# Strassen steps for four of the eight K tiles of the two remaining output blocks in an MLP's down projection

## The chip, the cores and the metric

The kernel runs on one core of one Trainium2 chip, as one program. The metric is the device time of one execution in microseconds. The kernel before takes 2032.7 us (median of three runs, 2032.12 to 2035.39). One further execution was recorded by the profiler: it took 2031.86 us, and its instructions span 2030.0 us.

The engines are named as in the profile: PE is TensorE (PEld its weight loads), DVE is VectorE, ACT is ScalarE, POOL is GpSimd, SP is SyncE, whose queue issues nearly all loads.

## The reference

A decoder trunk with two layers over 256 positions and a model width of 2048, all in float32. Layer 0 has a gated short convolution, layer 1 a latent attention; each is followed by a squared-ReLU MLP with a hidden width of 8192 and by a DeepNorm layer norm. The change concerns the MLPs alone, of which there are two:

```python
def sq_relu_mlp(x, w1, w2):
    return jnp.square(jax.nn.relu(x @ w1)) @ w2

def reference(...):
    ...
        h = layer_norm(ALPHA * h + mix, ln_g[layer, 0], ln_b[layer, 0])
        h = layer_norm(ALPHA * h + sq_relu_mlp(h, mlp_w1[layer], mlp_w2[layer]),
                       ln_g[layer, 1], ln_b[layer, 1])
```

`x` is 256 x 2048, `w1` 2048 x 8192 and `w2` 8192 x 2048.

## The kernel before

**Precision.** Every operand of a matrix product is kept in two parts: a high part, a rounded copy made by ACT, and a low part, the difference made by DVE (`split`, L116 and L117). A product is then three matmuls, high x high, high x low and low x high (`dot`, L276 to L278). So every weight tile of 128 x 1024 that is loaded costs one ACT copy and one DVE subtraction before PE can use it.

**The MLP by stages.** The hidden width is cut into NQ = 8 stages of QC = 8 chunks of 128 (`mlp`, L557). In each stage q the *up* part makes the eight hidden chunks: `products` multiplies the activations by `w1`, `whole` (L332, L333) joins the parts of the result, ACT applies ReLU and square (L597, L598), and the chunk is split again (`put_split`, L337, L338). The *down* part multiplies the eight chunks, which are now eight K tiles, by `w2` and adds to the accumulator `acc`, 2 token halves x 2048 columns, taken as NB = 4 blocks of 512 columns. `put` (L581) adds one finished PSUM tile of 128 x 512 to a block of `acc` on DVE.

**Strassen in the stages q = 1 to 6 (`FAST`).** Two neighbouring K tiles, the two token halves and the blocks 0 and 1 make a 2 x 2 by 2 x 2 product. It is computed in Winograd's form with seven products in place of eight (`FACTORS`, `down_fast`). The left operands S1 to S4 are made from the hidden chunks on DVE (L605 to L608) and split into `forms`. The right operands T1 to T4 are made from the weights in `prepare`: two raw tiles hold the four sub-blocks, a third tile `raw_t` holds T1 and T3 (L149), T2 replaces a sub-block (L152), and T4 (L155) replaces another. The three tiles and half a tile for T4 are then split. The seven products accumulate in seven PSUM tiles over the four pairs of K tiles, and `combine` adds them to the four blocks and token halves with eleven DVE instructions and one ACT copy. Blocks 2 and 3 are computed plainly by `down`, a block at a time.

**What sets the order of the work.** All weight tiles stand in one list, `stream`, in the order of their use. `take` hands out the next tile and prepares tiles ahead of it (load, ACT copy, DVE subtraction), up to LOOK = 5 units, where a plain tile is one unit and a pair of Strassen tiles three (`size`). Raw tiles come from a pool of five buffers, high and low parts from pools of eight each. A load can start when a raw buffer is free, which is when DVE has made the low part from it. The order on each engine is fixed when the program is built; each engine takes its instructions in that order and waits where an operand or a buffer is not ready. PSUM has eight banks, used in rotation.

**Other places that the change touches.** `late_constants` loads the identity, the rotary tables and the mask after the convolution (L356 to L359). In the second MLP, `turn_residual` transposes the residual on PE and adds it to a block of `acc`, before the last block of stages 1 to 4. `to_out` loads the gain and bias of the last norm on POOL's queue (L914), computes the last down part, normalises and stores.

Of the kernel before, what the change touches and what calls it, by code (L numbers as in the profile page):

```python
# [16 lines left out]
P = 128  # L17
# [17 lines left out]
NB = 4  # L35
BW = D // NB
FAST = range(1, NQ - 1)
FIRST = (0, 1, 2, 4, 6, 8, 12, 16)
HEAD = 4
GROUP = 3  # L40
# [8 lines left out]

@with_exitstack  # L50
def trunk(ctx: ExitStack, tc: tile.TileContext, xT, vecs, w_first, w_in, w_out, w_kv, w_q, w_uk, w_uv,
          w_qn, w_qp, w_o, w1, w2, w2f, cosT, sinT, mask, ident, gb, out):
    nc = tc.nc
    PS = bass.MemoryType.PSUM
    const = ctx.enter_context(tc.tile_pool(name="const", bufs=1))
# [124 lines left out]
    def psum(name):  # L180
        return Banks.next().tile([P, 512], F32, tag="mm", name=name)
# [118 lines left out]
    def down_late(x, put, blocks):  # L300

        ws = {}
        for t in range(2):
            for n in blocks:
# [11 lines left out]
    def down_fast(x, forms):  # L316

        ps = {p: psum(f"ps_f{p}") for p, _, _ in FACTORS}
        n = len(x) // 2
        for j in range(n):  # L320
            b, = take(1)
            a = {"11": held(x[2 * j], 0), "12": held(x[2 * j + 1], 0), "22": held(x[2 * j + 1], 1)}
            for i in range(4):
                a[f"S{i + 1}"] = [forms[:, j, o, i * P:(i + 1) * P] for o in range(2)]
            for p, l, r in FACTORS:
                dot(ps[p], b[r], a[l], j == 0, j == n - 1)
        return ps

    def whole(ps, out):

# [8 lines left out]


    vec = const.tile([P, C_END], F32, name="vec")
    cos_t = const.tile([P, T], F32, name="cos_t")
    sin_t = const.tile([P, T], F32, name="sin_t")
    mask_t = const.tile([P, 3 * P], F32, name="mask_t")
    id_t = const.tile([P, P], F32, name="id_t")
    ones = const.tile([P, P], F32, name="ones")
    col = const.tile([P, 4], F32, name="col")
# [3 lines left out]
        nc.tensor.matmul(warm[:, :P], ones, ones, start=True, stop=True)  # L351
    nc.vector.memset(col[:, 0:1], 1.0 / D)
    nc.vector.memset(col[:, 1:2], 1.0 / RK)

    def late_constants():
        nc.sync.dma_start(id_t, ident)  # L356
        nc.sync.dma_start(cos_t, cosT)
        nc.sync.dma_start(sin_t, sinT)
        nc.sync.dma_start(mask_t, mask)  # L359

    def rsqrt(out, ve, amid=None):

# [169 lines left out]
    for m in range(NC):  # L532
# [17 lines left out]
        if m >= NC // 2:  # L550
            for k in range(2 * m - NC, 2 * m - NC + 2):
                ln.prepare(k)
    late_constants()
    ln.widen("a1", "a2")
    summed(ln, chain(products(1, z), lagged(NC - 1, z)), residual)

    def mlp(idx, ln, blocks, fast, begin=None, extra=None):  # L557

        xt = act.tile([P, NC, 2 * T], F32R, tag="b", name=f"xhl{idx}")
        xhl = [xt[:, k, :] for k in range(NC)]
        state["fast"] = fast
        todo = iter(range(NC))

        def normal():
            k = next(todo, None)
            if k is not None:
                ln.normal(k, xhl[k])  # L570

        def block(n, t):
            return acc[:, t, n * BW:(n + 1) * BW]

        def put(n, t, ps):
            if q == 0:
                nc.scalar.copy(block(n, t), ps)
                for _ in range(2):
                    normal()
            else:  # L580
                nc.vector.tensor_tensor(block(n, t), block(n, t), ps, ALU.add)  # L581

        for q in range(NQ):
            ht = act.tile([P, QC, 2 * T], F32R, tag="c", name=f"h{idx}_{q}")
            h = [ht[:, k, :] for k in range(QC)]
            forms = None
            if q in FAST:
                forms = act.tile([P, QC // 2, 2, 4 * P], F32R, tag="a2", name=f"forms{idx}_{q}")
            if q == NQ - 1 and begin:
                begin()  # L590
            pair = []

            def hidden(m, ps, evac, *func):
                f = tmp.tile([P, T], F32, tag="fh", name="fh", bufs=3)
                evac(ps, f, *func)
                if not func:
                    nc.scalar.activation(f, f, AF.Relu)  # L597
                nc.scalar.activation(f, f, AF.Square)  # L598
                put_split(h[m], f)
                pair.append(f)  # L600
                if forms is not None and m % 2:
                    (a11, a21), (a12, a22) = ((v[:, :P], v[:, P:]) for v in pair[-2:])
                    sf = fast.tile([P, 4, P], F32, tag="sf", name="sf")
                    s1, s2, s3, s4 = (sf[:, i, :] for i in range(4))
                    nc.vector.tensor_tensor(s1, a21, a22, ALU.add)  # L605
                    nc.vector.tensor_tensor(s3, a21, a11, ALU.subtract)
                    nc.vector.tensor_tensor(s2, s1, a11, ALU.subtract)
                    nc.vector.tensor_tensor(s4, a12, s2, ALU.subtract)  # L608
                    split(forms[:, m // 2, 0, :], forms[:, m // 2, 1, :], sf.rearrange("p i c -> p (i c)"))

            if q == 0:
                for m in range(QC):
                    if m < GROUP:
                        if m == 0:
# [12 lines left out]
                acc = act.tile([P, 2, D], F32, tag="a1", name=f"acc{idx}")  # L627
            else:
                for m, ps in enumerate(products(QC, xhl, turned=None if q == NQ - 1 and begin else TURNED)):
# [12 lines left out]
    def combine(put, p):  # L642

        put(0, 1, p["4"])
        put(0, 0, p["2"])
        put(1, 0, p["3"])
        v, u = (raws.tile([P, 2, BW], F32, tag="raw", name="vu")[:, i, :] for i in range(2))
        put(0, 0, p["1"])
        nc.scalar.copy(v, p["1"])
        nc.vector.tensor_tensor(v, v, p["6"], ALU.add)  # L650
        nc.vector.tensor_tensor(u, v, p["7"], ALU.add)
        put(1, 0, v)
        put(0, 1, u)
        put(1, 0, p["5"])
        put(1, 1, u)
        put(1, 1, p["5"])

    def to_wide(block, put, h):

# [28 lines left out]
    with tc.tile_pool(name="att", bufs=1) as ap:  # L688
        lat = act.tile([P, 2 * NK, 2 * T], F32R, tag="c", name="lat")
        chl, qhl = ([lat[:, k, :] for k in range(o, o + NK)] for o in (0, NK))  # L690
        kpe = ap.tile([P, 2, T], F32, name="kpe")
        nc.gpsimd.memset(kpe, 0.0)
        rc = ap.tile([P, 2], F32, name="rc")
# [4 lines left out]
        def rope(dst, src, rows):  # L698

            a = tmp.tile([P, T], F32, tag="sq", name="ropea")  # L700
            b = tmp.tile([P, T], F32, tag="nu", name="ropeb")
# [198 lines left out]
    summed(after, out_chunks(), residual)  # L900


    def turn_residual(block, n):
        if 0 <= n < NB:
            for t in range(2):
                ps = psum("turned")
                for j in range(4):
                    nc.tensor.transpose(ps[:, j * P:(j + 1) * P], xres[:, 4 * n + j, t * P:(t + 1) * P], id_t)
                nc.vector.scalar_tensor_tensor(block(n, t), ps, ALPHA, block(n, t), ALU.mult, ALU.add)
# [153 lines left out]
```

## Time and profile before

| what | us |
|---|---|
| median of three runs | 2032.7 |
| profiled execution | 2031.86 |
| its span, first to last instruction | 2030.0 |
| PE busy | 2022.8 |
| PEld busy | 1763.4 |
| DVE busy | 1637.1 |
| ACT busy | 1186.2 |
| stages q = 1 to 6 of the first MLP, each of the first five | 85.78 |
| stages q = 1 to 4 of the second MLP, with the turned residual | 86.67 to 86.69 |
| stages q = 5 and 6 of the second MLP | 85.78 |

Busy time is the union of an engine's recorded instructions. For PE it says little, since the records of pipelined matmuls overlap. The granted TensorE clock is 1.000 throughout. In a group's line, the names are the program's tiles (out<-in), then come the shape and the count, busy time and the mean length of one; a line number can be that of a helper that many callers share.

### The profile page before, as it was taken

To read this page: it belongs to the slowest core of one execution; us is meant where nothing else is said; L and a number is where in the kernel's file an instruction comes from. 1 tells how busy PE (TensorE), PEld (TensorE's weight loads), DVE (VectorE), ACT (ScalarE), POOL (GpSimd) and SP (SyncE) were. 2 spreads that over 40 slices of the span, in tenths; PEclk is the share of its full clock that TensorE was granted. 3 is DMA by queue.
4 is the path that set the end of the run, shared out by engine and by line. 5 is a ranking of instruction groups with operands and counts; after the bars stand their busy time and mean duration, and the time that the engine had idled before them with its cause. 6 is when DMAs were issued, how large, how long until landed. Compare 5 with 4: busy or idle time off the path is not lost.

```text
span 2030.0 us, 30192 instructions
## 1 busy us (share of the span) xinstructions
PE 2022.8 (100%) x11240; PEld 1763.4 (87%) x11240; DVE 1637.1 (81%) x2559; ACT 1186.2 (58%) x1849; POOL 4.5 (0%) x25
## 2 busy tenths in 40 slices
PE   9999999999999999999999999999999999999998
PEld 8888888988888888888889998898888888888886
DVE  7667677778898988989788978776889898898966
ACT  6444445676566565655656655566656656565661
POOL 0000000000000000000000000000000000000000
PEclk9999999999999999999999999999999999999999
DMA  8666666564746557465654544656474664746573
GB/s 307 209 191 187 188 190 193 162 210 138 251 148 216 193 170 256 145 229 174 232 176 153 177 129 137 195 168 205 136 240 155 213 204 164 250 143 221 190 228 121
DMA packets 106851, 385.32 MB, mean 190 GB/s; under 512 B 11856, under 2 KB 12752, under 8 KB 106448
## 3 DMA queue, kind: packets, MB, share of 16 engines
q1 hardware_dynamic: 105984, 381.17, 57.9%
q0 software_dynamic: 576, 2.10, 0.3%
q8 instruction: 88, 1.44, 0.3%
q14 instruction: 59, 0.48, 0.1%
q10 hardware_dynamic: 144, 0.13, 0.0%
HBM read 381.25 MB, written 2.10 MB: 189 GB/s over the span
## 4 chain that ended last, share of the span: by engine, by line
PE 99%; DMA 0%; DVE 0%; issue 0%; SPq 0%; ACT 0%; DVEq 0%
PE ps_u L192 20%; PE ps_l L192 13%; PE ps_u L196 11%; PE ps_d L276 7%; PE ps_d L277 7%; PE ps_d L278 7%; PE ps_l L196 7%; PE ps_f L278 4%; PE ps_f L276 4%; PE ps_f L277 4%; PE ps_w L226 1%; PE ps_w L224 1%; PE ps_w L225 1%; PE ps_g L226 1%; PE ps_g L224 1%; PE ps_g L225 1%
## 5 line engine op out<-in xcount | busy, mean ns | idle before, releaser
L117 DVE TENSOR_TENSOR lo<-raw,hi 128x1024 fp32r<-128x1024 f32 x710 | 858.7, 1222 | 271.5 <-ACT hi L116 199.9
L116 ACT CAST hi<-raw 128x1024 fp32r<-128x1024 f32 x710 | 740.9, 1050 | 428.4 <-DMA raw<-in_w_dram 134.6
L192 PE MATMUL ps_u<-xhl,hi 128*128 128x512 f32 x1792 | 621.3, 391 | 0.0
L196 PE MATMUL ps_u<-xhl,lo 128*128 128x256 f32 x1792 | 500.1, 280 | 0.0
L192 PEld LDWEIGHTS ps_u<-xhl,hi 128*128 128x128 f32 x1792 | 334.4, 187 | 71.9
L196 PEld LDWEIGHTS ps_u<-xhl,lo 128*128 128x128 f32 x1792 | 339.2, 189 | 1.7
L276 PE MATMUL ps_d<-hi,h 128*128 128x512 f32 x640 | 249.9, 390 | 0.0
L277 PE MATMUL ps_d<-lo,h 128*128 128x512 f32 x640 | 249.3, 390 | 0.0
L278 PE MATMUL ps_d<-hi,h 128*128 128x512 f32 x640 | 249.2, 389 | 0.0
L192 PE MATMUL ps_l<-xhl_a,hi 128*128 128x512 f32 x704 | 244.1, 393 | 0.0
L196 PE MATMUL ps_l<-xhl_a,lo 128*128 128x256 f32 x704 | 195.5, 280 | 0.0
L192 PEld LDWEIGHTS ps_l<-xhl_a,hi 128*128 128x128 f32 x704 | 132.2, 188 | 29.8
L278 PEld LDWEIGHTS ps_d<-hi,h 128*128 128x128 f32 x640 | 120.2, 188 | 25.2
L276 PEld LDWEIGHTS ps_d<-hi,h 128*128 128x128 f32 x640 | 120.2, 188 | 25.0
L277 PEld LDWEIGHTS ps_d<-lo,h 128*128 128x128 f32 x640 | 120.2, 188 | 24.6
L196 PEld LDWEIGHTS ps_l<-xhl_a,lo 128*128 128x128 f32 x704 | 131.9, 188 | 0.2
L597 ACT ACTIVATE fh<-fh 128x256 f32<-128x256 f32 x112 | 46.5, 415 | 89.2 <-DVE fh L333 89.1
L116 ACT CAST hi_t<-raw_t 128x1024 fp32r<-128x1024 f32 x48 | 50.6, 1054 | 55.5 <-DVE raw_t L149 30.5
L192 PE MATMUL ps_l<-z,hi 128*128 128x512 f32 x240 | 82.4, 391 | 0.0
L226 PE MATMUL ps_w<-xd,hi 128*128 128x258 f32 x256 | 72.7, 285 | 0.0
L224 PE MATMUL ps_w<-xd,hi 128*128 128x258 f32 x256 | 72.6, 284 | 0.0
L225 PE MATMUL ps_w<-xd,lo 128*128 128x258 f32 x256 | 72.4, 283 | 0.0
(253 smaller groups left out, 3185.1 us busy)
## 6 DMA issues: line engine op xcount, KB each, us to landing
raw<-in_w_dram SPq DMA_DIRECT2D x416, 512.0 KB, 4.3
raw<-in_w2f_dram SPq DMA_DIRECT2D x96, 512.0 KB, 3.5
raw<-in_w_in_dram SPq DMA_DIRECT2D x88, 512.0 KB, 3.8
raw<-in_w_out_dram SPq DMA_DIRECT2D x32, 512.0 KB, 3.6
raw<-in_w_o_dram SPq DMA_DIRECT2D x32, 512.0 KB, 4.0
raw<-in_w_kv_dram SPq DMA_DIRECT2D x10, 512.0 KB, 3.6
raw<-in_w_q_dram SPq DMA_DIRECT2D x8, 512.0 KB, 4.4
raw<-in_w_uk_dram SPq DMA_DIRECT2D x8, 512.0 KB, 4.6
```

The costliest lines, as they stand in the source:

```text
L116: nc.scalar.copy(hi, src)
L117: nc.vector.tensor_tensor(lo, src, hi.bitcast(F32), ALU.subtract)
L192: nc.tensor.matmul(ps, w[blk // 8][0][:, blk % 8, :], x, start=first, stop=False)
L196: nc.tensor.matmul(ps[:, :T], w[blk // 8][1][:, blk % 8, :], x[:, :T], start=False, stop=last)
L224: nc.tensor.matmul(ps[:, :W], hi, x[k][:, :W], start=k == 0, stop=False)
L225: nc.tensor.matmul(ps[:, :W], lo, x[k][:, :W], start=False, stop=False)
L226: nc.tensor.matmul(ps[:, :W], hi, x[k][:, W:], start=False, stop=k == NC - 1)
L276: nc.tensor.matmul(ps, x[0], w[0], start=first, stop=False)
L277: nc.tensor.matmul(ps, x[0], w[1], start=False, stop=False)
L278: nc.tensor.matmul(ps, x[1], w[0], start=False, stop=last)
L597: nc.scalar.activation(f, f, AF.Relu)
```

## The change

In the stages q = 1 to 6, blocks 2 and 3 are no longer all plain. Their first four K tiles (two pairs, `PLAIN = QC // 2 - 2`) are still multiplied plainly, both blocks side by side; the last four (two pairs) go through the same seven products as blocks 0 and 1, from a new copy of the weights, `w2g`. Per stage this replaces four of the eight plain tiles by two pairs of Strassen tiles.

The seven products are no longer combined in each stage. Products "2", "3", "4" and a fourth tile, "22", in which only plain matmuls accumulate, are added straight to `acc`; the plain matmuls of the first four K tiles accumulate in the same PSUM tiles as "2", "3" and "4" (`fast_products` then goes on adding there). Products "1", "6", "7" and "5" (`OWN`) are added to side sums, `sums`, of 4 x 2 x 512 columns, at q = 1 copied there by ACT. `fold` adds the side sums to `acc` once, by eight DVE instructions of 1024 columns among the up products of stage 7. Each fast stage has 15 additions to `acc` or `sums` (8 of them ACT copies at q = 1).

To make room, several tiles move: two neighbouring hidden chunks share one tile and are split by one ACT and one DVE instruction of 512 columns; the rotary tables and the mask are loaded at the start of the attention; the gain and bias of the last norm are loaded on SP's queue. `turn_residual` now turns one token half at a time, behind each of the first two pairs of plain tiles.

```diff
+PLAIN = QC // 2 - 2
...
             out += halves(w1[l, q * QC:(q + 1) * QC])
-            lead = 0
-            if q in FAST:
-                out += [(w2f[l, q, j, 0], w2f[l, q, j, 1]) for j in range(QC // 2)]
-                lead = 2
-            out += halves(w2[l, q, lead:])
+            if q not in FAST:
+                out += halves(w2[l, q])
+                continue
+            out += [(w2f[l, q, j, 0], w2f[l, q, j, 1]) for j in range(QC // 2)]
+            for j in range(PLAIN):
+                out += halves(w2[l, q, 3, j]) + halves(w2[l, q, 2, j])
+            out += [(w2g[l, q, j, 0], w2g[l, q, j, 1]) for j in range(QC // 2 - PLAIN)]
...
+    OWN = ("1", "6", "7", "5")
...
+    def fast_products(ps, x, forms, j, fresh, last):
+        b, = take(1)
+        a = {"11": held(x[2 * j], 0), "12": held(x[2 * j + 1], 0), "22": held(x[2 * j + 1], 1)}
+        for i in range(4):
+            a[f"S{i + 1}"] = [forms[:, j, o, i * P:(i + 1) * P] for o in range(2)]
+        for p, l, r in FACTORS:
+            dot(ps[p], b[r], a[l], p in fresh, last)
...
+        sums = fast.tile([P, 4, 2, BW], F32, name=f"sums{idx}")
+        def keep(p, g, ps):
+            at = sums[:, OWN.index(p), g, :] if p in OWN else \
+                block(*{"2": (2 * g, 0), "3": (2 * g + 1, 0), "4": (2 * g, 1), "22": (2 * g + 1, 1)}[p])
+            if q == 1 and p in OWN:
+                nc.scalar.copy(at, ps)
+            else:
+                nc.vector.tensor_tensor(at, at, ps, ALU.add)
+        def down_pairs(h, forms):
+            n = QC // 2
+            ps = {p: psum(f"ps_f{p}") for p, _, _ in FACTORS}
+            for j in range(n):
+                fast_products(ps, h, forms, j, ps if j == 0 else (), j == n - 1)
+            for p in ps:
+                keep(p, 0, ps[p])
+            ps = {p: psum("ps_d") for p in ("22", "3", "2", "4")}
+            for j in range(PLAIN):
+                for nb, two in ((3, ((1, "22"), (0, "3"))), (2, ((0, "2"), (1, "4")))):
+                    w, = take(1)
+                    for t, p in two:
+                        for kk in range(2):
+                            k = 2 * j + kk
+                            dot(ps[p], wide_rows(w, kk), held(h[k], t), k == 0, p == "22" and k == 2 * PLAIN - 1)
+                if extra and q <= NB and j < 2:
+                    extra(block, q - 1, j)
+            keep("22", 1, ps["22"])
+            for p in OWN:
+                ps[p] = psum(f"ps_f{p}")
+            for j in range(PLAIN, n):
+                fast_products(ps, h, forms, j, OWN if j == PLAIN else (), j == n - 1)
+            for p in ("3", "2", "4", *OWN):
+                keep(p, 1, ps[p])
+        def fold():
+            s1, s6, s7, s5 = (sums[:, i] for i in range(4))
+            c = acc.rearrange("p t (g b c) -> p t b g c", g=2, b=2)
+            for d, a, b in ((c[:, 0, 0], c[:, 0, 0], s1), (s6, s6, s1), (c[:, 0, 1], c[:, 0, 1], s6), (s7, s7, s6),
+                            (c[:, 1, 0], c[:, 1, 0], s7), (c[:, 1, 1], c[:, 1, 1], s7),
+                            (c[:, 0, 1], c[:, 0, 1], s5), (c[:, 1, 1], c[:, 1, 1], s5)):
+                nc.vector.tensor_tensor(d, a, b, ALU.add)
+                yield
...
             def hidden(m, ps, evac, *func):
-                f = tmp.tile([P, T], F32, tag="fh", name="fh", bufs=3)
+                both = pair_tile(m) if forms is not None else None
+                f = both[:, m % 2, :] if forms is not None else tmp.tile([P, T], F32, tag="fh", name="fh", bufs=3)
...
-                put_split(h[m], f)
-                pair.append(f)
-                if forms is not None and m % 2:
+                if forms is None:
+                    put_split(h[m], f)
+                elif m % 2:
+                    at = ht[:, m - 1:m + 1, :]
+                    split(at[:, :, :T], at[:, :, T:], both)
...
+                    if q == NQ - 1:
+                        next(folds)
...
-                combine(put, down_fast(h, forms))
-            for n in range(2 if q in FAST else 0, NB):
-                if n == NB - 1 and extra:
-                    extra(block, q - 1)
-                down(h, put, n)
+                down_pairs(h, forms)
+            else:
+                for n in range(NB):
+                    down(h, put, n)
...
-            nc.gpsimd.dma_start(gbt[:, n, :], gb[n].partition_broadcast(P))
+            nc.sync.dma_start(gbt[:, n, :], gb[n].partition_broadcast(P))
```

More of the change, by code (lines that the diff above doesn't have):

```diff
@@ L591, in mlp, with pair_tile @@
             pair = []
+            def pair_tile(m):
+                if m % 2 == 0:
+                    pool = (act, "ab") if m % 4 else (fast, "fp")
+                    t = pool[0].tile([P, 2 * T], F32, tag=pool[1], name="fp")
+                    pair.append(t.rearrange("p (i t) -> p i t", i=2))
+                return pair[-1]
             def hidden(m, ps, evac, *func):
-                f = tmp.tile([P, T], F32, tag="fh", name="fh", bufs=3)
+                both = pair_tile(m) if forms is not None else None
+                f = both[:, m % 2, :] if forms is not None else tmp.tile([P, T], F32, tag="fh", name="fh", bufs=3)
                 evac(ps, f, *func)
@@ L598, in hidden @@
                 nc.scalar.activation(f, f, AF.Square)
-                put_split(h[m], f)
-                pair.append(f)
-                if forms is not None and m % 2:
-                    (a11, a21), (a12, a22) = ((v[:, :P], v[:, P:]) for v in pair[-2:])
+                if forms is None:
[3 more added lines that the diff above has]
+                    split(at[:, :, :T], at[:, :, T:], both)
+                    (a11, a21), (a12, a22) = ((both[:, i, :P], both[:, i, P:]) for i in range(2))
                     sf = fast.tile([P, 4, P], F32, tag="sf", name="sf")
@@ L690, in trunk @@
         chl, qhl = ([lat[:, k, :] for k in range(o, o + NK)] for o in (0, NK))
+        cos_t = ap.tile([P, T], F32, name="cos_t")
+        sin_t = ap.tile([P, T], F32, name="sin_t")
+        mask_t = ap.tile([P, 3 * P], F32, name="mask_t")
+        for t, source in ((cos_t, cosT), (sin_t, sinT), (mask_t, mask)):
+            nc.sync.dma_start(t, source)
         kpe = ap.tile([P, 2, T], F32, name="kpe")
@@ L900, in trunk, with turn_residual @@
     summed(after, out_chunks(), residual)
[L903 to L909, printed above, removed]
+    def turn_residual(block, n, t):
+        ps = psum("turned")
+        for j in range(4):
+            nc.tensor.transpose(ps[:, j * P:(j + 1) * P], xres[:, 4 * n + j, t * P:(t + 1) * P], id_t)
+        nc.vector.scalar_tensor_tensor(block(n, t), ps, ALPHA, block(n, t), ALU.mult, ALU.add)
     def to_out(block, put, h):
```

44 lines of the change are left out of this document (7 added, 37 removed).

## The prediction

> **What bounds the kernel now.** I read four views in this order: the busy times and the chain of waits on the page, what TensorE (PE) waited for, one stage cut into three windows, and VectorE's (DVE's) timeline around a seam of that stage.
>
> ```profile
> span 2030.0 us, 30192 instructions
> PE 2022.8 (100%) x11240; PEld 1763.4 (87%) x11240; DVE 1637.1 (81%) x2559; ACT 1186.2 (58%) x1849; POOL 4.5 (0%) x25
> PE 99%; DMA 0%; DVE 0%; issue 0%; SPq 0%; ACT 0%; DVEq 0%
> ```
>
> The chain that ended last is 99% PE. Busy PE is no proof, since records of pipelined matmuls overlap; the waits are:
>
> ```profile
> PE offset L961 <- DVE udiag L959: 1.2, 1, 1.2
> PE warm L351 <- DVE col L353: 1.1, 1, 1.1
> PE ps_g L192 <- ACT hi L116: 0.6, 1, 0.6
> PE lnAB L376 <- DVE rr L371: 0.3, 1, 0.3
> ```
>
> PE waited 3.2 us in all and never in a fast stage, so a matmul removed there is worth its full pitch as long as PE still finds its operands ready. Pitch is read from starts, not from the modelled 0.39 us:
>
> ```profile
> 498.86 0.39 PE L276 MATMUL ps_f<-t,h 128*128 128x512 f32 x1
> 505.86 0.40 PE L276 MATMUL ps_f<-hi,h 128*128 128x512 f32 x1
> ...
> 699.79 0.39 PE L277 MATMUL ps_d<-lo,h 128*128 128x512 f32 x1
> 711.58 0.39 PE L278 MATMUL ps_d<-hi,h 128*128 128x512 f32 x1
> ```
>
> Thirty steps of the fast product take 7.00 us (233.3 ns each), 52 plain steps 11.79 us (226.7 ns). A Strassen step is not only fewer matmuls: each is 6.6 ns dearer.
>
> ```profile
> 671.40:690.98 19.58, 19.58 (x86) 15.76 (x85) 18.37 (x25) 12.54 (x18) 0.00 (x0) 1.00 0.60 196
> 690.98:712.78 21.80, 21.80 (x99) 18.12 (x98) 19.32 (x24) 10.66 (x12) 0.00 (x0) 1.00 0.77 255
> 627.00:671.40 44.40, 44.40 (x257) 39.09 (x256) 36.80 (x58) 29.00 (x50) 0.00 (x0) 1.00 0.51 164
> sum 85.78, PE 85.78 PEld 72.97 DVE 74.49 ACT 52.20 POOL 0.00; mean PE 28.59 PEld 24.32 DVE 24.83 ACT 17.40 POOL 0.00
> ```
>
> The columns are stretch, length, then busy time of PE, PEld, DVE, ACT, POOL, granted clock (1.00), DMA share, GB/s. One fast stage (q = 3 of the first MLP) is 44.40 us of up products, 19.58 of fast products for blocks 0 and 1, and 21.80 of plain products for blocks 2 and 3. DVE is busy 74.49 of 85.78 us: 11.29 us of slack, the quantity on which all depends.
>
> **The sum.** *Matmuls.* A pair of K tiles of blocks 2 and 3 costs 24 plain matmuls, 24 x 226.7 = 5.44 us; by a Strassen step 21 matmuls, 21 x 233.3 = 4.90. That saves 0.54 us a pair, 1.08 a stage (2 pairs), and **13.0 us** for 12 stages. Neither the four plain tiles' new order nor the interleaved order in which the changed program issues the second half's products is in the trace. Should the 576 plain matmuls that stay take 233.3, that costs 3.8 us; should the 504 new Strassen matmuls take 226.7, it gains 3.3. I keep the rates of their own kinds.
>
> The Trainium skill (TensorE: Matmul & The Clock Gate, "Back-to-back issue gap") gives N/2.4 + 2.5 ns, 215.8 ns at 512 columns. By that the 72 matmuls would be worth an estimated 15.5 us and the two kinds would cost the same; the rows show 226.7 and 233.3, and the measurement decides.
>
> *DVE.* Two plain tiles of a pair need two low-part subtractions of 1.222 us. The Strassen pair needs three (L117), one raw_t (1.225), two half-size combinations (0.688, 0.690) and the T4 low part (0.686): 6.96 against 2.44, so 4.5 us more a pair and 9.0 a stage. Summed durations overrun busy time, because consecutive instructions overlap: one stage's add up to 82.1 against 74.49, a factor 0.907. So 8.2 us more. Splitting two hidden chunks at once (0.686 for 2 x 0.421, four times) gives back 0.3 to 0.6; I take 0.3. The accumulations stay 15 a stage (7 + 1 + 7 for 11 + 4), half of which now go to side sums; at q = 1 eight of them become ACT copies. New DVE work: 74.5 + 8.2 - 0.3 = **82.4 us** against a PE stage of 85.78 - 1.08 = 84.70. The slack falls from 11.3 to 2.3 us, 97% busy. ACT gains 2 x (1.05 + 0.62) us on 52.2 and stays near 55.
>
> *The seam.* Let E be the end of the fast products of blocks 0 and 1 (690.98 above).
>
> ```profile
> 688.08 0.68 DVE L581 TENSOR_TENSOR acc<-acc,ps_f 128x512 f32<-128x512 f32 x1
> 689.79 1.23 DVE L117 TENSOR_TENSOR lo<-raw,hi 128x1024 fp32r<-128x1024 f32 x1 [1.03 <-ACT hi L116]
> 690.93 0.68 DVE L581 TENSOR_TENSOR acc<-acc,ps_f 128x512 f32<-128x512 f32 x1
> 691.53 1.22 DVE L117 TENSOR_TENSOR lo<-raw,hi 128x1024 fp32r<-128x1024 f32 x1
> 692.66 1.28 DVE L581 TENSOR_TENSOR acc<-acc,ps_f 128x512 f32<-128x512 f32 x2
> ```
>
> Between these starts a 512-element instruction takes 0.60 us of the queue and a 1024-element one 1.14. The two accumulations from 692.66 on and three more end at 692.66 + 5 x 0.60, about E + 4.7. Then, in the changed program's order, come the first three steps of pair A (2.9 us, to E + 7.5) and the accumulation of product "22", which the third plain tile finishes at E + 2 x 2.72 + 1.36 = E + 6.8. Behind it stand pair A's remaining preparations: its second low part ends at E + 10.5, T4's high part (ACT) at E + 11.8, its low part at E + 12.8. PE arrives at E + 48 x 0.2267 = E + 10.9, begins with products that need the former, and wants T4's high part at E + 11.4. So it stalls 0.4 to 0.5 us; pair B then follows within a few tenths. Where the residual is turned (second MLP, q = 1 to 4), both sides shift by 0.9 us of transposes and 1.2 of DVE. I charge **0.45 us a stage, 5.4 us in all**; the ends are 0 and the 3.4 of the last rival but one. The wait on "22" has the rest of DVE's queue behind it. The skill states the reason in the same page ("Architectural detail": ACT and DVE are strict FIFO); the timeline above agrees, with DVE idle 1.03 us before a low part while a finished product waited.
>
> *What costs nothing.* The deferred folding is 8 instructions of 1.22 us in q = 7's up products (about 10 us a MLP): q = 7 needs no Strassen operands, so its DVE work is about 40 of 44.4 us; without that cover it would cost up to 20 us. The constants' loads move to a point where SP's queue has five tiles in flight. The gain/bias loads move from POOL's queue to SP's behind the last up product, ahead of the last four weight tiles: 2 MB at about 250 GB/s is 8 us, and PE reaches those tiles some 27 us later (3 half-blocks of 10.9 and 5.4 us), so nothing is late; the end of the program keeps its DVE tail.
>
> Sum: 2031.86 (the profiled execution; span 2030.0) - 13.0 + 5.4 = 2024.3. The median of the runs, 2032.7, is 0.8 above that execution, so I forecast **2025.1 us**.
>
> **Rivals.** *Clean overlap:* PE never stalls, since its product order at the seam is already bent around T4. For it: no wait in any stage before. Against: slack falls to a fifth. 2032.7 - 13.0 = 2019.7 us. *Balance:* stalls of 0.75 to 1.4 us a stage eat most of the saving, which is what a DVE at 98 to 99% would give: 2028.6 to 2036.8 us, middle 2032. *DVE becomes the bound:* one mechanism, the weight preparation of the fast stages. DVE lags some 7 us at the start of a stage's up products (five tiles, three and four accumulations after pair B) and must recover this out of idle time. Much of the old 11.3 us is waiting for tiles that PE has yet to free, and vanishes when DVE is late; the part in which ACT waits for a raw tile's load does not, since a late DVE frees the raw buffer late too. The stage takes 82.4 us plus what remains of idle time; beyond 3.4 us remaining, the kernel is slower than before. With 4.3 remaining, 86.7 a stage, +0.9 x 12 = 2043 us. For it: in the stage above ACT waited 9.8 us for such loads. Against: 5.8 of them lie in the plain stretch, where DVE had little else to do. *Not what it says:* were the new fast products priced like plain ones with one per pair still spared, the saving would be 16.3, within the range's low end.
>
> **How the numbers follow.** Forecast with stalls under 0.75 us 0.35, clean overlap 0.25: faster 0.60. Balance 0.22, DVE-bound 0.18. About 0.2% (4.1 us) is what a measurement here can tell from no change. The low end, 2017.5, takes in clean overlap and part of the 3.3 us on the fast pitch; the high end, 2037.5, takes in balance and leaves out most of the DVE-bound case. The likeliest case's own range is 2019 to 2028.6.
>
> **What would show it.** Right: matmuls of 512 columns fall by 72; the second half's 42 fast matmuls take 9.8 us; DVE is busy 82 to 83 us of a fast stage of 85.1; PE waits under 0.75 us a stage, on the T4 parts of pair A or B. Wrong: fast stages at or above 85.8 us, PE waiting on low parts of pairs in the first half too, or DVE idle over 3 us a stage in waits for ACT's high parts and for loads while PE waits.

## The result, and the profile after

The changed kernel takes 2041.87 us (median of six runs, 2040.30 to 2044.38), the kernel before 2031.98 beside it: a ratio of 1.0046 (95% interval 1.0033 to 1.0059). It is 9.9 us slower; the forecast was 7.6 faster, and 2041.87 lies above the range. The profiled execution took 2041.51 us, with a span of 2039.7. All 9.7 us of added span lie in the twelve fast stages: 2.2 in the first MLP (517.12 for 514.93) and 7.5 in the second (525.75 for 518.28). Here and below, times of a kernel are medians, and figures of stages, waits and single instructions are those of its one profiled execution.

Busy times and the chain of waits on the page of the changed kernel:

```profile
span 2039.7 us, 29958 instructions
PE 2019.8 (99%) x11168; PEld 1746.3 (86%) x11168; DVE 1730.4 (85%) x2631; ACT 1214.2 (60%) x1853; POOL 2.3 (0%) x21
PE 72%; DVE 18%; DMA 5%; issue 3%; ACT 2%; SPq 0%; ACTq 0%; DVEq 0%
```

There are 72 matmuls fewer, as forecast, and 93 us more of DVE work. Busy time doesn't show the loss; the chain does: PE's share fell from 99% to 72%. What PE waited for in the second MLP's six stages, and then in the first's:

```profile
PE ps_d L279 <- ACT t L119: 2.0, 3, 0.8
PE ps_u L195 <- ACT hi L119: 2.0, 1, 2.0
PE ps_f L279 <- DVE acc L584: 1.8, 1, 1.8
```

```profile
PE ps_d L279 <- ACT t L119: 3.5, 5, 0.8
PE ps_d L280 <- DVE t L120: 0.5, 1, 0.5
```

The `t` that ACT writes is T4's high part. This view names only the longer waits. By the matmuls' starts (gaps over 0.15 us beyond the pitch) PE lost 6.8 us in the first MLP and 10.4 in the second, and none before. One stage (q = 6 of the first MLP) in three windows (up products, blocks 0 and 1, blocks 2 and 3), with the columns as in the prediction:

```profile
885.43:929.85 44.42, 44.42 (x258) 39.15 (x257) 41.60 (x60) 31.46 (x49) 0.00 (x0) 1.00 0.62 217
929.85:949.41 19.56, 19.56 (x86) 15.68 (x85) 18.78 (x26) 12.05 (x17) 0.00 (x0) 1.00 0.63 189
949.41:971.80 22.39, 21.47 (x93) 16.95 (x92) 21.41 (x26) 10.81 (x12) 0.00 (x0) 1.00 0.50 163
sum 86.37, PE 85.45 PEld 71.78 DVE 81.79 ACT 54.32 POOL 0.00; mean PE 28.48 PEld 23.93 DVE 27.26 ACT 18.11 POOL 0.00
```

The part that lost six matmuls grew from 21.80 to 22.39 us. E, the start of PE's first matmul for blocks 2 and 3, is at 949.41:

```profile
949.17 0.40 PE L281 MATMUL ps_f<-hi_t,forms 128*128 128x512 f32 x1
949.41 0.40 PE L279 MATMUL ps_d<-hi,h 128*128 128x512 f32 x1
```

DVE's timeline in this part:

```profile
950.16 1.23 DVE L120 TENSOR_TENSOR lo<-raw,hi 128x1024 fp32r<-128x1024 f32 x1 [1.26 <-ACT hi L119]
951.30 1.28 DVE L584 TENSOR_TENSOR acc<-acc,ps_f 128x512 f32<-128x512 f32 x2
952.50 2.47 DVE L584 TENSOR_TENSOR sums<-sums,ps_f 128x512 f32<-128x512 f32 x4
954.89 1.22 DVE L120 TENSOR_TENSOR lo<-raw,hi 128x1024 fp32r<-128x1024 f32 x1
...
957.88 0.68 DVE L584 TENSOR_TENSOR acc<-acc,ps_d 128x512 f32<-128x512 f32 x1
...
960.75 0.69 DVE L158 TENSOR_TENSOR raw<-raw 128x512 f32<-128x512 f32 x1
```

ACT's and PE's timelines there:

```profile
961.52 0.62 ACT L119 CAST t<-raw 128x512 fp32r<-128x512 f32 x1 [1.24 <-DVE raw L158]
```

```profile
960.39 0.39 PE L279 MATMUL ps_d<-hi,h 128*128 128x512 f32 x1
960.89 0.50 PE L280 MATMUL ps_d<-lo,h 128*128 128x512 f32 x1
962.20 0.50 PE L279 MATMUL ps_d<-t,h 128*128 128x512 f32 x1 [0.81 <-ACT t L119]
```

DVE adds the first half's products until E + 5.5 and starts to make T4 at E + 11.3, ACT's high part ends at E + 12.7, and PE, which by the forecast wanted it at E + 11.4, starts at E + 12.8, having lost 1.1 us there and 0.3 on the matmul before.

### The profile page after: what moved, and what is told of

It is laid out like the page before. It is cut to its first block, busy times and chain, and to the rows that moved or that the text cites. A ratio compares the mean times of both kernels' runs of the same rounds, so it can differ in the third digit from the quotient of the medians.

```text
span 2039.7 us, 29958 instructions
## 1 busy us (share of the span) xinstructions
PE 2019.8 (99%) x11168; PEld 1746.3 (86%) x11168; DVE 1730.4 (85%) x2631; ACT 1214.2 (60%) x1853; POOL 2.3 (0%) x21
## 4 chain that ended last, share of the span: by engine, by line
PE 72%; DVE 18%; DMA 5%; issue 3%; ACT 2%; SPq 0%; ACTq 0%; DVEq 0%
PE ps_u L195 16%; PE ps_l L195 13%; PE ps_u L199 8%; PE ps_l L199 7%; DVE lo L120 6%; DMA raw<-in_w_dram 4%; PE ps_d L279 4%; PE ps_d L281 4%; PE ps_d L280 3%; DVE lo_t L120 2%; DVE raw_t L152 2%; PE ps_w L229 1%; PE ps_w L227 1%; PE ps_w L228 1%; ACT hi L119 1%
## 5 line engine op out<-in xcount | busy, mean ns | idle before, releaser
L279 PE MATMUL ps_d<-hi,h 128*128 128x512 f32 x472 | 184.9, 392 | 0.5 <-ACT hi L119 0.3
L280 PE MATMUL ps_d<-lo,h 128*128 128x512 f32 x472 | 184.6, 391 | 0.3
L281 PE MATMUL ps_d<-hi,h 128*128 128x512 f32 x472 | 184.0, 390 | 0.0
L119 ACT CAST hi_t<-raw_t 128x1024 fp32r<-128x1024 f32 x72 | 75.7, 1051 | 129.4 <-DVE raw_t L152 113.3
L279 PEld LDWEIGHTS ps_d<-hi,h 128*128 128x128 f32 x472 | 88.6, 188 | 21.0 <-ACT hi L119 1.8
L280 PEld LDWEIGHTS ps_d<-lo,h 128*128 128x128 f32 x472 | 88.6, 188 | 20.8 <-DVE lo L120 2.5
L281 PEld LDWEIGHTS ps_d<-hi,h 128*128 128x128 f32 x472 | 88.6, 188 | 18.4
L152 DVE TENSOR_TENSOR raw_t<-raw,raw 128x1024 f32<-128x1024 f32 x72 | 87.6, 1217 | 7.0 <-DMA raw<-in_w2f_dram 7.0
L120 DVE TENSOR_TENSOR lo_t<-raw_t,hi_t 128x1024 fp32r<-128x1024 f32 x72 | 87.7, 1219 | 2.4 <-ACT hi_t L119 1.9
L195 PE MATMUL ps_l<-z,hi 128*128 128x512 f32 x240 | 82.4, 391 | 0.0
L645 ACT ACTIVATE fp<-fp 128x256 f32<-128x256 f32 x96 | 39.9, 416 | 68.7 <-DVE fp L334 68.6
L229 PE MATMUL ps_w<-xd,hi 128*128 128x258 f32 x256 | 72.7, 285 | 0.0
```

What stands on the lines that cost most here:

```text
L119: nc.scalar.copy(hi, src)
L120: nc.vector.tensor_tensor(lo, src, hi.bitcast(F32), ALU.subtract)
L152: nc.vector.tensor_tensor(t.rearrange(two, a=2), b12.unsqueeze(1).to_broadcast([P, 2, BW]), r1.rearrange(two, a=2), ALU.subtract)
L195: nc.tensor.matmul(ps, w[blk // 8][0][:, blk % 8, :], x, start=first, stop=False)
L229: nc.tensor.matmul(ps[:, :W], hi, x[k][:, W:], start=False, stop=k == NC - 1)
L279: nc.tensor.matmul(ps, x[0], w[0], start=first, stop=False)
```

## The experiments

Three theories stand against each other. **Queue:** PE waits for the DVE and ACT work of the Strassen operands (a variant: DVE is simply full). **Banks:** in stages 1 to 4 of the second MLP the two turned tiles and the second half's eight share eight PSUM banks (the second half is the work on blocks 2 and 3), so that a product waits until DVE has emptied another's bank. **Pace:** the up products, on which the diff changes nothing, run at either of two paces, 346.7 or 353.3 ns for a pair of a 512- and a 256-column matmul (44.39 or 45.2 us an up part), without any wait. Stages 1 to 7 of the two MLPs have fourteen such parts, twelve of them in the fast stages. Before, all ran at the first pace; in the changed kernel four ran at the second (q = 2 of the first MLP, q = 3, 4 and 5 of the second). Each time below stands beside its ratio to the kernel before, with the 95% interval.

**e1, one pair in place of two.**

```diff
-PLAIN = QC // 2 - 2
+PLAIN = QC // 2 - 1
```

> PLAIN is 3 instead of 2: only one pair of K tiles of blocks 2 and 3 takes the Strassen step, everything else of the change stays. Queue theory (TensorE starves because VectorE's queue, 97% busy, brings the operands of the seam too late): VectorE falls to about 78 of 85 us a stage, TensorE's waits fall to under 0.3 us a stage, and the saving of 36 matmuls (6.5 us) comes through: 2026 to 2029 us. Pace theory (the loss lies in TensorE, whose matmuls run at a longer pitch in the new mix whatever VectorE does): half of the saving and half of the loss go, so the time lies half way between the two kernels, 2035 to 2039 us.

2041.69 us, 1.0048 (1.0033 to 1.0063). Gaps fell from 17.2 to 6.2 us in all, but ten of the fourteen up parts now ran at 353.3, for four: six more, 6 x 0.82 = 4.9 us. With the 6.5 us of matmuls that are not saved, this takes back the 11.0 us of the gaps. Neither expectation held, because both moved at once.

**e2, the residual turned at the end of the stage.**

```diff
-                if extra and q <= NB and j < 2:
-                    extra(block, q - 1, j)
+            for t in range(2):
+                if extra and q <= NB:
+                    extra(block, q - 1, t)
```

> The residual is turned after the second half's products instead of between its plain tiles, so that no more than eight PSUM tiles are open there. Bank theory (in stages 1 to 4 of the second MLP ten tiles share eight banks, and TensorE waits for the release of product 3): waits on accumulations go from stages 2 and 3 of the second MLP, 3 to 6 us, so 2036 to 2039 us, all of it in the second MLP. If the banks play no part: 2040 to 2043 us, and stages 2 and 3 of the second MLP stay above 89 us.

2034.65 us, 1.0014 (1.0004 to 1.0023). By the median, the place of eight transposes a stage is worth 7 us, more than was expected. The trace doesn't show where: the profiled execution (2038.35 us) was 3.7 slower than the median, and its second MLP took 525.81 us, as in the changed kernel. There the up products behind the transposes waited 3.0 us for DVE's additions. The first MLP, which the edit leaves alone, had gaps of 3.8 us for 6.8: single executions differ by that much.

**e3, without the low parts of the left operands.**

```diff
-                    split(at[:, :, :T], at[:, :, T:], both)
+                    nc.scalar.copy(at[:, :, :T], both)
```

> Leaves out a part of the computation: in stages 1 to 6 the low parts of the hidden chunks and of the S operands are not made, and TensorE reads the high part in their place. TensorE's instructions stay the same in number and size, VectorE loses eight instructions of 512 columns a stage, about 4.8 us of its queue, and no load or buffer is touched. Queue theory: TensorE's waits fall to under 0.4 us a stage and the matmuls saved come through, 2020 to 2027 us. Pace theory: nothing that TensorE does has changed, 2039 to 2043 us.

2030.12 us, 0.9991 (0.9982 to 1.0001). With less on DVE the first MLP's gaps fall from 6.8 to 1.2 us. The second MLP keeps 4.5 us in stages 2 and 3, of which 1.4 are waits for DVE's additions and 2.2 a wait of the next up part for its first weight tile. This fits the queue theory, but can't tell a full DVE from one late operand.

**e4, three additions for T1 to T4 on GpSimd.**

```diff
-        nc.vector.tensor_tensor(t4, b21, b12, ALU.subtract)
+        nc.gpsimd.tensor_tensor(t4, b21, b12, ALU.subtract)
```

(and the two others likewise)

> The three additions that make the T operands (L152, L155, L158) run on GpSimd, which is idle, instead of VectorE, which loses six times 2.3 us a stage, about 14 us, and comes to 67 of 85 us. Queue theory, if GpSimd takes no more than about twice VectorE's time for them: 2019 to 2024 us, since VectorE's load is the cause. Rival: GpSimd is slower than that (over 14 us a pair) or slows VectorE when both run, and its results become what the seam waits for: 2045 us or more.

2203.88 us, 1.0849 (1.0824 to 1.0873). Groups of instructions of this kernel (count, then busy time and mean ns):

```profile
L152 POOL TENSOR_TENSOR raw_t<-raw,raw 128x1024 f32<-128x1024 f32 x72 | 203.8, 2831 | 1222.8 <-DMA raw<-in_w2f_dram 622.0 <-DVE fp L334 424.3 <-DMA raw<-in_w2g_dram 121.7
L120 DVE TENSOR_TENSOR t<-raw,t 128x512 fp32r<-128x512 f32 x72 | 97.6, 1355 | 0.0
L584 DVE TENSOR_TENSOR sums<-sums,ps_f 128x512 f32<-128x512 f32 x80 | 49.4, 678 | 0.0
```

GpSimd takes 2831 ns where DVE took 1217, and T4's low part on DVE grows from 682 to 1355 ns in the mean. That mean hides two cases: 36 of the 72 ran wholly beside a GpSimd instruction and took 2033 ns, the other 36 took 677. The additions of PSUM tiles took 678 beside GpSimd (30 of them) and 677 without it. PE waited 80 us for T4's low part and 22 for its high part; the granted clock was 0.975 here. The Trainium skill ("SBUF — State Buffer", "SBUF: two separate sides") says that GpSimd and a DVE instruction with two SBUF inputs take one port pair from each other for a whole instruction. The trace agrees: 2033 for 677 ns with two SBUF inputs, 678 for 677 with a PSUM input.

**e5, the pace alone, in the kernel before.**

```diff
-                for m, ps in enumerate(products(QC, xhl, turned=None if q == NQ - 1 and begin else TURNED)):
+                for m, ps in enumerate(products(QC, xhl, turned=None)):
```

> The kernel before with one edit: in the stages 1 to 6 of both MLPs the up products no longer swap the high and the low matmul of the third K tile. Same matmuls, same operands, same DVE and ACT work; only the order of two matmuls in each of twelve up parts differs. Pace theory (the up products run at 346.7 or at 353.3 ns a pair, set by how PE enters the part; 128 pairs, so 0.85 us a part): if the swap is what brings them to 346.7 after the even 227 ns of the plain products, the twelve up parts take 45.2 us and the time is 2032.0 + 12 x 0.85 = 2042. If the even 227 ns entry alone does it, 2032.0. Queue theory (every microsecond over the forecast is a wait of PE for DVE or ACT): 2032.0, as no wait changes.

2042.32 us, 1.0049 (1.0032 to 1.0066). The order of two matmuls in each of thirteen up parts (the edit reaches stage 7 of the second MLP too), with no wait added, costs 10 us. All thirteen ran at the longer pace. The same stage as in the prediction (q = 3), by windows:

```profile
627.78:672.99 45.21, 45.21 (x257) 39.23 (x256) 38.19 (x59) 29.14 (x49) 0.00 (x0) 1.00 0.54 175
672.99:692.50 19.51, 19.51 (x87) 15.84 (x86) 17.34 (x24) 12.43 (x17) 0.00 (x0) 1.00 0.60 182
692.50:714.30 21.80, 21.80 (x98) 18.01 (x96) 19.46 (x23) 10.91 (x11) 0.00 (x0) 1.00 0.75 250
```

With 257 records in the up part in both kernels, a clock of 1.00 and PE busy throughout, the up part takes 45.21 us for 44.40. The pace is shown by itself, 0.81 us a part.

**e6, the swapped K tile elsewhere in each stage** (on e1).

```diff
+                at = {1: TURNED, 2: None, 3: 7, 4: 1, 5: 3, 6: 4} if idx == 1 else {1: None, 2: 5, 3: 6, 4: 8, 5: 9, 6: 12}
```

> The kernel with one pair of Strassen steps in blocks 2 and 3 (measured at 2041.7, ten of its twelve up parts at 353.3 ns a pair), with the swapped K tile of the up products at another place in each stage: 2, none, 7, 1, 3, 4 in the first MLP and none, 5, 6, 8, 9, 12 in the second. Pace theory: the up parts that the swap brings to 346.7 are 0.85 us shorter, the others stay at 45.2 us; 2041.7 less 0.85 for each, so 2033 to 2041, and the trace tells which places do it. Queue theory: the waits, 6.2 us in all in the kernel with one pair, set the time, 2041 to 2042 whatever the place.

2042.73 us, 1.0054 (1.0040 to 1.0069). In the first MLP the part without a swap behind a Strassen pair fell to 44.38 us; those with swaps at 7, 1, 3 and 4 stayed at 45.2. Behind plain products it is the reverse: with the swap 44.39, without it 45.21. In the second MLP, where the turned residual stands in between, swaps at 8 and 9 gave 347.1 ns a pair, those at 5, 6 and 12 about 353. So the swap doesn't bring one pace; it can also take PE out of the better one. The time lies above the range of the pace theory, which had let the swap only help.

**e7, the residual turned among the up products.**

```diff
-                if extra and q <= NB and j < 2:
-                    extra(block, q - 1, j)
...
+                    elif extra and q <= NB and m in (3, 5):
+                        extra(block, q - 1, (m - 3) // 2)
```

> The changed kernel, with the turned residual of the second MLP moved out of the plain products of blocks 2 and 3 into the up products of the same stage (behind products 3 and 5), where no Strassen tile holds a bank. Nothing is left out. Bank theory (the two turned tiles and the eight tiles of the second half share eight banks, so that products wait for DVE's additions): the waits of 4.6, 2.5 and 2.2 us in the second MLP go and the time is 2033 to 2036, below or near that of turning them at the end of the stage (2034.7). Queue theory: DVE has the same work, so only what the banks had cost can go; waits of 0.5 to 1.9 us a stage stay in the first MLP, sum near 6.8 us. Pace theory: the transposes among the up products can bring the rest of a part to another pace, 0 to 0.6 us in each of four stages.

2034.03 us, 1.0007 (0.9998 to 1.0016). The second MLP's gaps fall from 10.4 to 4.2 us, the first's from 6.8 to 5.4. Stages 2 and 3 go from 7.1 us of gaps to 0.25. So the place of the transposes is what cost them; the banks are a part of it, as the account below shows.

**e8, the change without its Strassen steps.**

```diff
-PLAIN = QC // 2 - 2
+PLAIN = QC // 2
```

(and `fold` for blocks 0 and 1 alone, with half the columns)

> The changed kernel without its Strassen steps in blocks 2 and 3: all eight K tiles are multiplied plainly there, the two blocks side by side, the four side sums are still kept and folded for blocks 0 and 1. It has as many matmuls as the kernel before, so none of the 13.0 us are saved; DVE has four additions and the two extra pairs' splits and sums less than the changed kernel. Queue theory: PE waits for nothing, 2032 to 2034. Pace theory: the up parts are entered from the even 227 ns of the plain products, as before, all at 346.7, so 2032 to 2034 too. Bank theory: the turned residual shares banks with eleven tiles here as well, so 0.5 to 2 us a stage in four stages of the second MLP, 2034 to 2040.

2035.13 us, 1.0014 (1.0004 to 1.0023). All up parts ran at 346.7, with gaps of 1 us in all. The time lies in the range of the bank theory, but its waits do not appear: the second MLP's gaps are 0.2 us. The profiled stages are 1.3 and 1.0 us longer per MLP than before: about 3 us is the price of side sums, half the fold and interleaving, and the larger loss belongs to the Strassen steps.

**e9, blocks 2 and 3 in the order in which operands are made** (on the changed kernel; T4's product last).

```diff
+    AS_MADE = tuple(sorted(FACTORS, key=lambda f: "3175264".index(f[0])))
...
-            for p in ("3", "2", "4", *OWN):
+            for p, _, _ in AS_MADE:
```

> The changed kernel with one edit: in blocks 2 and 3 the seven products of a pair are issued in the order in which DVE and ACT make their operands (3, 1, 7, 5, 2, 6, and 4, which needs T4, at the end), and are added to the sums in that order. No work is added or left out. Seam theory (PE waits because product 4 comes first and needs T4, which is made last; the rest of DVE's work would fit): the need for T4 moves 18 matmuls x 233 ns = 4.2 us back, the eight waits on T4's high part (5.6 us) and the smaller ones beside them go, the first MLP's six stages fall from 517.1 to 511-514 us, and the time is 2033 to 2037, as the banks of the second MLP stay as they are. Rival, DVE bound (DVE is late by its whole load, whatever product asks first): the waits move to other products, 2040 to 2043. Pace theory: some up parts may be entered in another pattern, up to 0.85 us each either way.

2040.11 us, 1.0040 (1.0027 to 1.0054). By the total, the full DVE (the rival, 2040 to 2043) seemed right. By stages it is not: in the first MLP's stages 1 to 5 PE waits nowhere, and its gaps fall from 6.8 to 0.8 us, with DVE's load unchanged. Its six stages take 513.3 us, as the seam theory expected. Five of its up parts now run at 353.3 in place of one (+3.3 us), and the second MLP keeps 10.2 us of gaps.

**e10, the same order on e7.**

> The same order of products in blocks 2 and 3, on the kernel whose turned residual stands among the up products (2034.0). Seam theory: its waits of 0.4 to 1.4 us a stage (9.6 us in twelve stages) fall below 0.3 a stage, 2025 to 2029. DVE bound: 2033 to 2036. Pace theory: up to 0.85 us a stage either way on top of it, from the pattern in which PE leaves the second half.

2029.81 us, 0.9990 (0.9981 to 0.9999). PE has no wait left in the second MLP's six stages and 0.8 us in the first's. A stage's seam (q = 4, E at 775.27) on ACT and on PE:

```profile
786.82 0.62 ACT L119 CAST t<-raw 128x512 fp32r<-128x512 f32 x1 [1.24 <-DVE raw L158]
```

```profile
786.20 0.40 PE L279 MATMUL ps_d<-hi,forms 128*128 128x512 f32 x1
...
790.39 0.40 PE L279 MATMUL ps_d<-t,h 128*128 128x512 f32 x1
```

T4's high part still ends at E + 12.2; PE starts the pair at E + 10.9 and asks for T4 at E + 15.1. The DVE that was thought full is busy 82.3 of 85.4 us here. What is left is the pace: eleven up parts, those of stage 7 of the second MLP among them, are entered at 353.3.

**e11, one pair, in that order, without swaps in stages 2 to 7.**

```diff
+PLAIN = QC // 2 - 1
+                for m, ps in enumerate(products(QC, xhl, turned=None if q > 1 else TURNED)):
```

> One pair of Strassen steps in blocks 2 and 3 in place of two (6.5 us of matmuls saved, not 13.0), the turned residual among the up products, the products of that pair in the order of their operands, and no swapped K tile in the up products of the stages 2 to 7. Pace theory: one pair leaves PE in the pattern from which the unswapped up part ran at 346.7 ns a pair, so eleven up parts of 44.4 us; with the waits of DVE's queue gone, stages of 85.3 us, 2025 to 2030. If the order of the pair's products changes the pattern in which PE leaves it, up to 0.85 us more a stage, 2034 to 2039. Queue theory alone: 2041.7 less the bank waits of 4 us, 2036 to 2038.

2037.59 us, 1.0028 (1.0018 to 1.0039). The second branch: with T4's product last PE leaves the pair in another pattern, from which the unswapped parts took 45.23 us too. The time alone would also fit the queue theory; the trace decides, with gaps of 1.0 us in all and eleven of the twelve unswapped parts at 353.3 throughout.

**e12, that order in blocks 0 and 1 as well** (on e10).

> As the run before the last, with the products of blocks 0 and 1 in the order of their operands as well. Seam theory: in the first half no wait stood in any stage, so within 2 us of the run with the second half alone, 2024 to 2031. DVE bound: 2033 to 2036. A rival of its own: the first half's products now finish in another order, so that the bank of the next part comes free later, and PE waits there up to 0.7 us a stage, 8 us in all.

2029.49 us, 0.9988 (0.9979 to 0.9998): as e10. The order mattered only at the seam.

**e13, the swap at k = 4** (on e10). The starts in e10 and e11 gave a rule: the 353.3 pace is a cycle of three pairs, with starts 232 118, 240 120, 236 114 ns apart, and a swap ends it when it follows the pair 232 118.

```diff
+                at = {} if q == NQ - 1 and begin else {0: TURNED if q == 1 else 4}
+                if extra and q <= NB:
+                    at[4] = 2
```

> The kernel with the products of blocks 2 and 3 in the order of their operands and the turned residual among the up products (2029.8), with the swapped K tile of the up products moved from k = 2 to k = 4 in the stages 2 to 7, and one more swap at k = 2 of the product behind the first turned half. Same matmuls. Pace theory, now with a rule read from the traces: the 353.3 pace is a cycle of three pairs (232 118, 240 120, 236 114), and a swap behind the pair 232 118 ends it (121 237 235 117, then 230 117 for good), one behind another pair does not; there k = 4 stands behind 232 118 in stages entered as those are now. So the up parts of stages 2 to 6 of the first MLP fall from 45.2 to 44.4 us, those of stages 5 to 7 of the second too, and stages 1 to 4 there by 0.2 to 0.8: 6 to 8 us in all, 2021.5 to 2024. If the position makes no difference, 2029 to 2031. A rival between: PE reaches the seam 0.8 us earlier in each stage, and the waits come back there, 2024 to 2028.

2026.55 us, 0.9975 (0.9966 to 0.9985): 5.4 us below the kernel before. The first MLP's stages:

```profile
453.93:538.60 84.67, 84.67 (x431) 71.75 (x430) 71.14 (x95) 53.22 (x80) 0.00 (x0) 1.00 0.50 159
538.60:624.63 86.03, 85.67 (x432) 71.44 (x431) 78.15 (x104) 53.73 (x78) 0.00 (x0) 1.00 0.58 189
624.63:709.32 84.69, 84.69 (x432) 71.82 (x431) 81.79 (x110) 54.32 (x77) 0.00 (x0) 1.00 0.60 201
709.32:794.01 84.69, 84.69 (x432) 71.82 (x430) 82.44 (x111) 54.34 (x77) 0.00 (x0) 1.00 0.58 199
794.01:878.78 84.77, 84.77 (x431) 71.66 (x430) 81.01 (x109) 53.55 (x76) 0.00 (x0) 1.00 0.58 196
878.78:964.96 86.18, 86.00 (x433) 72.13 (x431) 82.78 (x111) 55.05 (x78) 0.00 (x0) 1.00 0.61 200
```

Where nothing is late a stage takes 84.67 to 84.69 us. The gain fell short of 6 to 8 us, and the time lies in the range of the rival between. Gaps of 0.4 to 0.8 us came back in four stages, and in three up parts (the last row's among them) a hold of some 0.1 us just ahead had shifted the cycle, so that the swap came behind another pair and left them at 353.3.

**e14, the swap at five places.**

```diff
+                at = {} if q == NQ - 1 and begin else {0: TURNED if q == 1 else {2: 1, 3: 3, 4: 4, 5: 5, 6: 7}.get(q, 4) if idx == 1 else 4}
```

> The same, with the swap in the first MLP's stages 2 to 6 at k = 1, 3, 4, 5 and 7. By the rule (a swap behind the pair 232 118 only, which recurs every three K tiles) 1, 4 and 7 bring their stages to 346.7 ns a pair and 44.4 us, 3 and 5 leave theirs at 353.3 and 45.2; the time is 1.7 us above that of the run with 4 throughout. Without the rule (any swap, or none, or the entry alone decides) all five are alike.

2027.86 us, 0.9984 (0.9975 to 0.9993). k = 1 and 4 gave 44.40 and 44.41 us, 3 and 5 gave 45.21 and 45.20. k = 7 gave 45.22, against the expectation: there a hold of 0.08 us ahead of the part had shifted the cycle, and the swap came behind 241 120. So the pair ahead of the swap decides, and not the place alone: in the first products of e13 and e14, 20 of 20 swaps behind 232 118 (to within 2 ns) led to 346.7, and 6 of 6 behind another pair did not. The rule is not complete. One of the 20 stood behind 230 117 (q = 2 of e14) and led to 346.7; in the changed kernel a swap behind 230 117 (q = 2 of the first MLP) led to 353.3. There the pair alone doesn't decide, and no run isolates what does.

## Why the prediction was wrong

- **Matmuls, right.** 72 are gone, and a stage without a wait and at the first pace takes 84.67 us for 85.78: 1.11 saved, where 1.08 was forecast.
- **DVE's load, right.** 82.4 us of a stage were forecast; stages 3 to 6 of the first MLP show 81.5 to 81.8, those of e10 82.3. "DVE becomes the bound", with 86.7 a stage and 2043 us, came nearest in time and is refuted as a mechanism: e10 carries the same load, and PE's gaps are 0.8 us in all twelve stages.
- **The seam, the step that failed first.** The wait and its place are right (T4's high part, wanted at E + 11.4); the charge, "0.45 us a stage, 5.4 us in all", is not. Gaps of 0.5 to 1.9 us a stage came, 6.8 us in the first MLP and 3.3 in stages 1 and 4 to 6 of the second, 10.1 in all. What failed is E. The forecast put "the end of the fast products of blocks 0 and 1" at 690.98. In the same trace PE starts the plain products 0.97 us earlier:

```profile
689.78 0.39 PE L278 MATMUL ps_f<-hi_t,forms 128*128 128x512 f32 x1
690.01 0.40 PE L276 MATMUL ps_d<-hi,h 128*128 128x512 f32 x1
```

  All three windows of that stage lie late by as much (its up part starts at 626.03, not 627.00), which leaves their lengths right and every "E +" of DVE and ACT 0.97 too small, while PE's own steps are counted from E. With E at 690.01 the same working has the additions end at E + 5.65 and T4's high part at E + 12.8. The stage shown above has E + 5.5 and E + 12.7, and in the seven full seams without a turned residual (stages 2 to 6 of the first MLP, 5 and 6 of the second) the high part ended at E + 11.8 to E + 13.0. Against a need at E + 11.4 that is 1.4 us a stage, about 16.4 us for twelve, and 2036 us: the case that the prediction called Balance and gave 0.22. So DVE did what was forecast; PE comes to the seam 0.97 us earlier than it was read.
- **The turned residual, the second step that failed.** "Both sides shift" left out what else hangs on the transposes' place. Stages 2 and 3 of the second MLP lost 7.1 us. Of these 2.6 are waits for a PSUM bank. In stage 2 a product waits 1.78 us for DVE's addition of a tile of the same half, which stands in DVE's queue behind two low parts:

```profile
1587.13 2.35 DVE L120 TENSOR_TENSOR lo<-raw,hi 128x1024 fp32r<-128x1024 f32 x2
1589.40 0.68 DVE L584 TENSOR_TENSOR acc<-acc,ps_d 128x512 f32<-128x512 f32 x1
```

```profile
1590.13 0.50 PE L279 MATMUL ps_f<-hi_t,forms 128*128 128x512 f32 x1 [1.78 <-DVE acc L584]
```

  In stage 3 the next up part loses 2.2 us, waiting for its first weight tile. ACT copies that tile when its load has landed, and the load was issued at 1675.02, just when DVE's low part that starts at 1673.78 had ended:

```profile
1673.78 1.22 DVE L120 TENSOR_TENSOR lo_t<-raw_t,hi_t 128x1024 fp32r<-128x1024 f32 x1
1678.80 1.04 ACT L119 CAST hi<-raw 128x1024 fp32r<-128x1024 f32 x1 [1.89 <-DMA raw<-in_w_dram]
1679.89 0.50 PE L195 MATMUL ps_u<-xhl,hi 128*128 128x512 f32 x1 [2.01 <-ACT hi L119]
```

  The other 2.3 us are smaller waits, mostly for parts of T4 and of weights. Moving the residual away takes 7 to 8 us by the medians (e2, e7) without touching DVE's work, and e7's trace has the gaps of both stages gone. Neither the tiles that share banks nor the late load were counted in the prediction.
- **The pitch.** The prediction weighed the pitches of plain and Strassen matmuls and took the up products' as given. Four up parts at 353.3 cost 3.3 us in the changed kernel; in e1, e10 and e11 this term is the largest.
- **The sum.** The twelve stages took 1042.9 us, 22.7 over the 1020.2 of a clean overlap (before, less 13.0): 17.2 of gaps, 3.3 of pace, and 2.2 of delays below 0.15 us each and of second-half pitch, not resolved further. Of these 5.4 had been charged.

Why PE has two paces is open. The runs show that the pattern of the matmuls before has a part in selecting one and that it lasts until something breaks it; they don't show what in PE keeps it.

## What to carry to other kernels

When two engines meet at a point, read that point for both from the starts of their own instructions: here 0.97 us in one start was twice the wait that was forecast. Before a queue is called full, compare the order in which it makes operands with the order in which they are asked for: here the same load cost 6.8 us of waits in six stages or 0.8. Whatever is placed between two uses of PSUM takes part in the rotation of banks, so count the tiles that are open at once (2.6 us of waits here). Where PE is the bound, read its pitch from the starts in every stage, on the parts that an edit doesn't touch too, and compare by stage: a total can hide two changes of several us each that cancel (e1, e9).

## What the runs showed of the hardware

- The same matmuls run at 346.7 or 353.3 ns a pair (1.9% apart) at a granted clock of 1.00 without a wait, and swapping the order of two neighbours can move PE from one to the other, either way (e5, e6, e13, e14).
- The difference, 6.6 ns, is also that between the plain matmuls (226.7 ns) and the Strassen ones (233.3). By the formula of the Trainium skill (TensorE: Matmul & The Clock Gate, "Back-to-back issue gap"), N/2.4 + 2.5 ns, a matmul of 512 columns would take an estimated 215.8 ns, less than both.
- A DVE subtraction of 512 columns with both inputs in SBUF took three times as long wholly beside a GpSimd instruction (2033 ns for 677); an addition with a PSUM input did not change (678 for 677) (e4).
